# Which engine waits for the last store: SyncE or GpSimd

## Chip, cores, metric

One core of a Trainium2 chip. The metric is the device time of one execution in microseconds, the median of several runs. It is longer than the span that the profile shows (first to last instruction of the program): in this kernel by about 1.34 us.

## The reference

```python
def setup_inputs():
    batch, dim = 1024, 4096
    return {"x": randn(batch, dim) as float32, "y": randn(batch, dim) as float32}

def reference(x, y):
    z = x * y
    return (0.5 * z * (1 + np.tanh(np.sqrt(2 / np.pi) * (z + 0.044715 * z ** 3)))).astype(np.float32)
```

(Shortened.) Two arrays of 16.8 MB are read, multiplied, put through GELU, and one array of 16.8 MB is written.

## The kernel before

The data is cut into three pieces. SyncE issues every transfer; VectorE multiplies in place, ScalarE applies GELU in place; each transfer has a semaphore of its own. GpSimd has no part in it. What matters is the end:

```python
    # ... loads, multiplications and activations cut ...
    for i, (a, b) in enumerate(STORES):
        if i == 0:
            nc.sync.wait_ge(sem_y[-2], 16)
        nc.sync.wait_ge(sem_act, done[b])
        nc.sync.dma_start(out=columns(out, a, b), in_=xs[:, a:b]).then_inc(sem_o[i], 16)   # L113
    for i in range(len(STORES) - 1):
        nc.sync.wait_ge(sem_o[i], 16)                                                      # L115
    nums = sorted(s.num for s in [*sem_x, *sem_y, *sem_o[:-1], sem_mul, sem_act])
    assert nums == list(range(nums[0], nums[-1] + 1))
    nc.sync.sem_clear(range(nums[0], nums[-1] + 1))                                        # L118
    nc.sync.wait_ge(sem_o[-1], 16).then_inc(sem_o[-1], -16)                                # L119
```

While the last store is in flight SyncE already clears all the other semaphores; then it waits for the last store and takes its 16 off again. In the trace `sem_o[-1]` is semaphore 109.

## Time and profile before

| | |
|---|---|
| device time, median of 3 runs | 119.75 us (119.73 to 119.86) |
| device time and span of the profiled run | 119.64 and 118.3 us |
| landings of the two large stores | 98.970 and 116.763 us |
| last store: issue / landing | 97.487 / 118.270 us |
| last instruction of the program (SyncE, L119) ends | 118.304 us |
| last update of semaphore 2 | 119.757 us |

The prediction below shows the page's lines and reads them. By "landing" is meant the last of the sixteen increments that the trace has for each of the nine transfers. Two kinds of record matter. The views of instructions show the program's own instructions; the last wait appears there as 17 ns at 118.3 us, when it is over, although SyncE had waited 1.4 us. The semaphore records give number and time of the updates of semaphores, and they go on after the program's last instruction: five more steps of semaphore 2 (118.447 to 118.612 us), writes to nearly all other semaphores (118.572 to 119.177, 0.61 us), nine steps of semaphore 2 (119.401 to 119.757). These stand in the trace and not on the page. The records name no engine and no purpose.

A pass means here nine steps of semaphore 2, as from 119.401 to 119.757 us. The first pass at the end has its first four steps before the landing (2.147 to 97.658 us) and the five at 118.447 to 118.612 after it. The recorded texts call a pass "barrier", the order of its steps "serpentine", the time from one step to the next "hop" and the five blocks of writes "reset". Which engine makes which step, and that each writes a block, is the reading of the times.

### The profile page before, as it was taken

How to read it: one execution, taken by the hardware profiler on the slowest of the kernel's cores; microseconds unless marked ns; L12 is line 12 of the kernel's file. 1: busy time of each engine (PE TensorE's matmuls, PEld its weight loads, DVE VectorE, ACT ScalarE, POOL GpSimd, SP SyncE). 2: the span in 40 equal slices, each digit the busy share in tenths (PEclk: the TensorE clock that was granted, in tenths of full speed). 3: DMA queues.
4: the chain of work that ended last, by engine and by line, in shares of the span. 5: the costliest groups of instructions: out<-in, count | busy, mean ns of one | idle time of the engine just before them, and what ended most of it. 6: DMA issues, size and time to landing. Idle time of an engine off the chain costs nothing.

```text
span 118.3 us, 82 instructions
## 1 busy us (share of the span) xinstructions
DVE 35.2 (30%) x13; ACT 31.0 (26%) x14; POOL 0.2 (0%) x4
## 2 busy tenths in 40 slices
DVE  0000000000000069999920000059999940000000
ACT  3000000000000001977974000007998990000000
POOL 0000000000000000000000000000000000000000
DMA  9988899889988897797797797798899888977975
GB/s 375 556 355 355 355 643 421 355 355 421 643 355 355 355 654 327 327 654 327 327 654 327 327 654 327 327 576 355 355 576 487 355 355 368 613 327 327 654 327 222
DMA packets 1296, 50.33 MB, mean 425 GB/s; under 512 B 144, under 2 KB 144, under 8 KB 528
## 3 DMA queue, kind: packets, MB, share of 16 engines
q1 hardware_dynamic: 1296, 50.33, 98.8%
HBM read 33.55 MB, written 16.78 MB: 425 GB/s over the span
## 4 chain that ended last, share of the span: by engine, by line
DMA 53%; DVE 24%; ACT 3%; issue 1%; DVEq 0%
DMA ys<-in_y_dram 53%; DVE xs L96 24%; ACT xs L104 3%; DVEq L93 0%
## 5 line engine op out<-in xcount | busy, mean ns | idle before, releaser
L96 DVE TENSOR_TENSOR xs<-xs,ys 128x2048 f32<-128x2048 f32 (+3 forms) x13 | 35.2, 2778 | 60.7 <-DMA ys<-in_y_dram 60.7
L104 ACT ACTIVATE xs<-xs 128x2048 f32<-128x2048 f32 (+3 forms) x13 | 29.7, 2301 | 64.5 <-DVE xs L96 64.5
L104 ACT ACT_TABLE_LOAD x1 | 1.3, 1283 | 1.9 <-PEq L59 1.9
L134 POOL MEMSET const-bfloat16-1.0<- 128x1 bf16 x1 | 0.1, 102 | 0.0
L134 POOL MEMSET const-uint8-127<- 128x1 uint8 x1 | 0.1, 102 | 0.0
L134 POOL MEMSET const-float32-0.0<- 128x1 f32 x1 | 0.1, 99 | 0.2 <-issue 0.2
L134 POOL MEMSET const-float32-1.0<- 128x1 f32 x1 | 0.1, 99 | 0.0
## 6 DMA issues: line engine op xcount, KB each, us to landing
xs<-in_x_dram SPq DMA_DIRECT2D x1, 7552.0 KB, 57.9
ys<-in_y_dram SPq DMA_DIRECT2D x1, 7552.0 KB, 22.5
out_dram<-xs SPq DMA_DIRECT2D x1, 7552.0 KB, 20.4
xs<-in_x_dram SPq DMA_DIRECT2D x1, 640.0 KB, 3.6
ys<-in_y_dram SPq DMA_DIRECT2D x1, 640.0 KB, 19.7
out_dram<-xs SPq DMA_DIRECT2D x1, 640.0 KB, 20.8
xs<-in_x_dram SPq DMA_DIRECT2D x1, 22.6
ys<-in_y_dram SPq DMA_DIRECT2D x1, 40.4
```

Of the source, the lines that this page charges most:

```text
L96: nc.vector.tensor_mul(out=xs[:, c : c + w], in0=xs[:, c : c + w], in1=ys[:, r + c - a : r + c - a + w],).then_inc(sem_mul, 1)
L104: nc.scalar.activation(out=xs[:, c : c + w], in_=xs[:, c : c + w], func=GELU).then_inc(sem_act, 1)
L134: nc = _bacc.Bacc("TRN2", target_bir_lowering=False, num_devices=1)
```

## The change

The last wait goes from SyncE to GpSimd, which has been idle since the start (0.2 us of work there). The idea is that SyncE's program ends with the clear, and an engine with nothing else to do stands guard.

```diff
     nc.sync.sem_clear(range(nums[0], nums[-1] + 1))
-    nc.sync.wait_ge(sem_o[-1], 16).then_inc(sem_o[-1], -16)
+    nc.gpsimd.wait_ge(sem_o[-1], 16).then_inc(sem_o[-1], -16)
```

## The prediction

> **What bounds the kernel now.** I read the page first: span, busy shares, DMA queue and the DMA issues.
>
> ```profile
> span 118.3 us, 82 instructions
> DVE 35.2 (30%) x13; ACT 31.0 (26%) x14; POOL 0.2 (0%) x4
> ...
> q1 hardware_dynamic: 1296, 50.33, 98.8%
> HBM read 33.55 MB, written 16.78 MB: 425 GB/s over the span
> ...
> out_dram<-xs SPq DMA_DIRECT2D x1, 640.0 KB, 20.8
> ```
>
> The one DMA queue is busy for 98.8% of 16 engines' span. VectorE and ScalarE work for under a third of it, GpSimd for 0.2 us at the start. So the kernel is 50.33 MB through the DMA engines. The last store takes 20.8 us from issue to landing although it has only 640 KB, because it stands behind the two large stores.
>
> Next, the order of time at the end (start, duration, engine), then the waits of SyncE's sequencer (total, times, longest).
>
> ```profile
> 93.66 3.80 ACT L104 ACTIVATE xs<-xs 128x2048 f32<-128x2048 f32 x3 [0.29 <-DVE xs L96]
> 94.41 1.49 DVE L96 TENSOR_TENSOR xs<-xs,ys 128x1280 f32<-128x1280 f32 x1
> 96.33 1.49 SPq L113 DMA_DIRECT2D out_dram<-xs  x2
> ```
>
> ```profile
> SPq L115 <- DMA out_dram<-xs: 18.9, 1, 18.9
> ...
> SPq L119 <- SPq L119: 1.4, 1, 1.4
> ```
>
> All computing and issuing is over by 97.82 us (96.33 + 1.49). For the remaining 20.5 us SyncE only waits: 18.9 us for the large stores, then 1.4 us at line 119, the wait that the change moves. The view names SyncE itself as the releaser of that last wait, but the releaser must be the landing of the last store: the trace's semaphore records have its sixteenth increment at 118.270 us. The two lines in question, by source line (duration in ns min/median/max, first and last start):
>
> ```profile
> L118 SPq EVENT_SEMAPHORE_RANGE_CLEAR  x1: 44/44/44, 116.8 to 116.8; - x1
> ```
>
> ```profile
> L119 SPq EVENT_SEMAPHORE  x1: 17/17/17, 118.3 to 118.3; - x1
> ```
>
> The clear is already done 1.4 us before the last wait ends. Nothing the program does on SyncE follows the wait, so there is nothing to take off SyncE's path.
>
> The device time is longer than the span: the profiled execution took 119.64 us against 118.3, so about 1.34 us outside the program's own instructions belongs to the time. The views say nothing of it, but the trace keeps semaphore updates until 119.757 us. After the last instruction I see in them: semaphore 2 stepping five times (118.447, 118.492, 118.530, 118.564, 118.612); nearly all other semaphores written once each, in five blocks of about 50 that overlap, the first from 118.572 and the last until 119.177; then semaphore 2 stepping nine times (119.401 to 119.757). This is where the change can act.
>
> [...] the undisturbed last pass takes 119.757 − 119.401 = 0.356 us in nine steps. [...] Here the last increment is at 118.270 and the waiting instruction starts at 118.287, 17 ns later[...].
>
> **The change, part by part.**
> Removed from SyncE: one 17 ns instruction after a wait. Added to GpSimd: the same instruction; GpSimd has been idle since the start. Moved: nothing else. No transfer is issued at another time, no buffer comes free earlier, and the DMA stream that fixes 118.270 us is untouched. So the span should stay at 118.3, and only the way from 118.270 to the end can change.
>
> First, the order of the serpentine. Semaphore 2 steps at 2.147, at 97.576, 97.614, 97.658, and then not until 118.447. One engine arrives at 2.147, when only TensorE and GpSimd have finished. The second waits for ScalarE, whose last update is at 97.471. VectorE had finished earlier (last update 95.908) and did not step before ScalarE did, so it stands behind it. SyncE is fifth: its step follows the end of line 119. I read it as TensorE, ScalarE, GpSimd, VectorE, SyncE, and back: VectorE, GpSimd, ScalarE, TensorE. The hops of one engine repeat up and down: ScalarE 34, GpSimd 39 and 38, VectorE 44. That TensorE is the end post and GpSimd in the middle is a choice: the last hop is the slowest (47 ns), and TensorE's semaphore instructions are the slow ones, 51 ns against 17, in these lines:
>
> ```profile
> L59 POOLq EVENT_SEMAPHORE  x4: 17/17/17, 1.4 to 1.8; - x4
> ...
> L59 PEldq EVENT_SEMAPHORE  x2: 51/51/51, 1.5 to 1.9; - x2
> ```
>
> Before: SyncE is the turning point. The four ahead of it have stepped by 97.658, and only the way back remains: 118.612 − 118.447 = 0.165 us.
>
> After: GpSimd is the late one. TensorE and ScalarE have stepped; SyncE and VectorE have finished but may not step before GpSimd. So from GpSimd's step there is VectorE up, SyncE, VectorE down, GpSimd, ScalarE, TensorE. The undisturbed passes show that stretch: 119.757 − 119.473 = 0.284 us in the last one, and −0.302 to −0.003, so 0.299, in the one just before the program. Difference: 0.119 to 0.134 us later.
>
> Second, the way from landing to the late engine's step. SyncE: 17 ns to notice, 17 to the update at 118.304, 143 to its step at 118.447; in all 177. GpSimd, from its three waits at the start: 24 ns to notice (1.050 to 1.074, 1.378 to 1.402, 1.705 to 1.729) and 25 to the update (1.074 to 1.099 and so on). Then the step to the barrier: from a barrier step to the first semaphore write of its own block SyncE takes 118.572 − 118.447 = 125 ns and GpSimd, by the order above, 118.670 − 118.530 = 140. I estimate 143 × 140/125 = 160, and 140 as the low end. In all 189 to 209, so 12 to 32 ns more than SyncE.
>
> The sum is 0.131 to 0.166 us; I take 0.15. It goes to the end in full[...]. 119.75 + 0.15 = 119.90 us, 0.13% more.
>
> **The rivals.**
> A. SyncE, relieved of the wait, comes to the end early, and the closing work overlaps with the last store. For it: SyncE's own 143 ns from its last instruction to the barrier would be hidden. Against it: GpSimd has to pay the same step instead[...]. If GpSimd's step were free it would be about −0.143 + 0.12, nearly nothing; 119.6 at the very best, should GpSimd not stand in the way of the barrier.
> B. I have TensorE and GpSimd the wrong way round, and GpSimd opens and closes the serpentine. Then all nine steps come after the landing: 0.356 in place of 0.165, so +0.19 and the entry on top, about 119.96.
> C. Only the end of the program's own instructions counts, or noise covers it: 119.75 to 119.78. The 1.34 us between time and span speaks against the first; the spread of the three runs, 0.13 us, is as large as the effect, so the second can't be excluded in one comparison.
> D. A long wait of 116 us on GpSimd wakes slower than the short ones seen at its start. Nothing in the trace shows one; 0.1 us more would make 120.0.
>
> **Range and chances.** The centre is 119.90. Below it lie A, C and a draw at the low end of the spread; above it B, D and a draw at the high end. I give 119.74 to 120.06. Two per cent is 2.4 us, some sixteen times the effect and more than everything after the landing (1.49 us), so within 2% is all but sure: 0.98, with 0.01 on each side for something unseen in the DMA stream.
>
> **What would show it.** In the changed profile the last instruction should be GpSimd's semaphore instruction at 118.3 us, about 24 ns after the landing, with the span unchanged to within run-to-run scatter, and SyncE's last one the clear near 116.8. Semaphore 2 should step twice by 97.62 (TensorE, ScalarE) and seven times after the landing, where before it stepped four and five times; the first of the seven 0.19 to 0.21 us after the landing, and from there 0.284 to 0.299 to the last. One early step and eight late ones, or none and nine, would mean that I have the order wrong. If the landing itself moves by more than 0.1 us, the difference in time is the DMA's and not the wait's. A time below 119.7 would sink the argument.

The sum came to 0.131 to 0.166 us, of which 0.119 to 0.134 for the steps that remain and 0.012 to 0.032 for the way to the step; taken was 0.15. The 160 ns for GpSimd's step in it are an estimate. That the difference reaches the end in full was an assumption before the result.

## The result, and the profile after

The changed kernel takes 120.37 us (median of 6 runs, 120.25 to 120.46); the kernel before 119.78 us (6 runs, 119.73 to 120.46, of which five lie below 119.87). Ratios here are the mean time of one kernel's fast runs over that of the other's in the same rounds, so not quite the ratio of those medians: 1.0039, 95% interval 1.0017 to 1.0061. It is slower, by well under the 2% that would count, but four times as much as predicted and outside the predicted range.

The page of the changed kernel looks the same:

```profile
span 118.5 us, 82 instructions
DVE 35.2 (30%) x13; ACT 31.0 (26%) x14; POOL 0.2 (0%) x4
...
q1 hardware_dynamic: 1296, 50.33, 98.8%
HBM read 33.55 MB, written 16.78 MB: 425 GB/s over the span
...
out_dram<-xs SPq DMA_DIRECT2D x1, 640.0 KB, 20.8
```

The order of time at its end, then SyncE's waits (the line for 119 is gone), then lines 118 and 119:

```profile
93.86 3.80 ACT L104 ACTIVATE xs<-xs 128x2048 f32<-128x2048 f32 x3 [0.29 <-DVE xs L96]
94.61 1.49 DVE L96 TENSOR_TENSOR xs<-xs,ys 128x1280 f32<-128x1280 f32 x1
96.53 1.49 SPq L113 DMA_DIRECT2D out_dram<-xs  x2
```

```profile
SPq L115 <- DMA out_dram<-xs: 18.9, 1, 18.9
```

```profile
L118 SPq EVENT_SEMAPHORE_RANGE_CLEAR  x1: 44/44/44, 117.0 to 117.0; - x1
```

```profile
L119 POOLq EVENT_SEMAPHORE  x1: 17/17/17, 118.5 to 118.5; - x1
```

Every duration is that of before. All is shifted by about 0.2 us, and most of this offset is there long before the change acts: the first large load of x landed at 22.992 us before and 23.144 after. That is scatter of the transfers, as a repeat shows below.

The difference is in the semaphore records after the last landing. In each pass semaphore 2 makes nine steps, which the prediction reads as up through the engines and back down. These are the times in us of the steps of the first pass, with the last landing and the last update of semaphore 109; the bar separates the steps before the landing from those after it:

```
          landing  update   | steps of semaphore 2
before    118.270  118.304  | 2.147 97.576 97.614 97.658 | 118.447 118.492 118.530 118.564 118.612
after     118.452  118.502  | 2.147 97.772 | 119.055 119.098 119.122 119.218 119.258 119.292 119.339
```

From the landing to the end of the pass (called the tail below): 118.612 − 118.270 = 0.342 us before, 119.339 − 118.452 = 0.887 us after, so 0.545 more. What follows, the writes and the second pass, is unchanged: 119.757 − 118.612 = 1.145 and 120.487 − 119.339 = 1.148 us. Two steps come early and seven late, as predicted, and those seven take 0.284 us, as predicted. But the first of the seven comes 0.553 us after GpSimd's update; SyncE's came 0.143 us after its own.

### The profile page after: what moved, and what is told of

The parts are those of the page before. It is cut to its first block, busy times and chain, and to the rows that moved or that the text cites. A ratio compares the mean times of both kernels' runs of the same rounds, so it can differ in the third digit from the quotient of the medians.

```text
span 118.5 us, 82 instructions
## 1 busy us (share of the span) xinstructions
DVE 35.2 (30%) x13; ACT 31.0 (26%) x14; POOL 0.2 (0%) x4
## 4 chain that ended last, share of the span: by engine, by line
DMA 53%; DVE 24%; ACT 3%; issue 1%; DVEq 0%
DMA ys<-in_y_dram 53%; DVE xs L96 24%; ACT xs L104 3%; DVEq L93 0%
## 5 line engine op out<-in xcount | busy, mean ns | idle before, releaser
L96 DVE TENSOR_TENSOR xs<-xs,ys 128x2048 f32<-128x2048 f32 (+3 forms) x13 | 35.2, 2779 | 60.9 <-DMA ys<-in_y_dram 60.9
```

Source lines behind the costliest of these rows:

```text
L96: nc.vector.tensor_mul(out=xs[:, c : c + w], in0=xs[:, c : c + w], in1=ys[:, r + c - a : r + c - a + w],).then_inc(sem_mul, 1)
```

## The experiments

Theory T1: on its way from its program's last instruction to its step of semaphore 2 GpSimd has some 0.4 us of its own that SyncE has not, whatever it waited for. Rivals: the moved clear or wait costs in itself (T2), the half microsecond belongs to the pass itself, when the others have arrived (T3), GpSimd wakes slowly after 116 us of idleness (T4), every engine but SyncE pays it (T5), an instruction has to be fetched at the end of the program, and the cost depends on where that lies (T6). All runs gave correct results.

### GpSimd waits, but for an earlier store

```diff
-    for i in range(len(STORES) - 1):
-        nc.sync.wait_ge(sem_o[i], 16)
-    nums = sorted(s.num for s in [*sem_x, *sem_y, *sem_o[:-1], sem_mul, sem_act])
+    nc.sync.wait_ge(sem_o[0], 16)
+    nums = sorted(s.num for s in [*sem_x, *sem_y, sem_o[0], sem_mul, sem_act])
 ...
     nc.sync.sem_clear(range(nums[0], nums[-1] + 1))
+    nc.gpsimd.wait_ge(sem_o[1], 16).then_inc(sem_o[1], -16)
     nc.sync.wait_ge(sem_o[-1], 16).then_inc(sem_o[-1], -16)
```

> SyncE keeps the wait for the last store; GpSimd waits only for the second store (lands near 116.8 us) and SyncE clears before that. Theory T1 (GpSimd's own way from its last instruction to the barrier takes about 0.55 us, whatever it waited for): GpSimd's step of semaphore 2 comes 0.55 us after its update, near 117.4, hidden behind the last store; from the last landing to the end of the first barrier pass 0.34 us as before, device time that of before (119.8 us, ratio 1.000). Theory T2 (moving the clear or any wait off SyncE costs in itself): time near 120.3. Theory T3 (the 0.55 us belongs to the pass of the barrier, when GpSimd holds the others up after they arrived): GpSimd's step follows its update within 0.16 us, near 117.0.

Measured: 119.79 us against 119.76 before, ratio 0.9998 (0.9983 to 1.0013). Line 118 of this run's kernel, by source line:

```profile
L118 POOLq EVENT_SEMAPHORE  x1: 17/17/17, 116.9 to 116.9; - x1
```

GpSimd's update is at 116.912 us and its step of semaphore 2 at 117.465: 0.553 us again, with nobody to wait for and nobody behind it in a hurry. The last store lands at 118.377, so the step is long over; from landing to the end of the pass it takes 0.339 us. T2 and T3 fall. The half microsecond is GpSimd's own and costs nothing as long as GpSimd is not the last.

### Two waits in a row on GpSimd

```diff
-    nc.sync.wait_ge(sem_o[-1], 16).then_inc(sem_o[-1], -16)
+    nc.gpsimd.wait_ge(sem_o[-1], 16)
+    nc.gpsimd.wait_ge(sem_o[-1], 16).then_inc(sem_o[-1], -16)
```

> As the changed kernel, but GpSimd waits for the last store twice in a row, and only the second wait takes the 16 off. T1 (own way to the barrier after the program's last instruction): the second wait starts about 0.08 us after the first, and the step of semaphore 2 still comes 0.55 us after its update; time 0.08 us above the changed kernel. T4 (slow waking of the sequencer after a wait of 116 us): the second wait starts 0.4 us or more after the first, and the step then follows within 0.16 us; time as the changed kernel.

The profile still has 82 instructions: the two waits had been merged into one with two conditions (43 ns in place of 17), so the spacing of the two was not to be seen. It took 120.41 us, the step came 0.553 us after the update once more. For T4 this run decides nothing.

### GpSimd at work shortly before the end

GpSimd waits for the second store, zeroes a few elements of the spent y buffer, then waits for the last store.

```diff
     nc.sync.sem_clear(range(nums[0], nums[-1] + 1))     # without sem_o[1], as in the first experiment
-    nc.sync.wait_ge(sem_o[-1], 16).then_inc(sem_o[-1], -16)
+    nc.gpsimd.wait_ge(sem_o[1], 16).then_inc(sem_o[1], -16)
+    nc.gpsimd.memset(ys[:, 0:8], 0.0)
+    nc.gpsimd.wait_ge(sem_o[-1], 16).then_inc(sem_o[-1], -16)
```

> GpSimd waits for the second store, sets 8 elements a partition of the spent y buffer to zero, then waits for the last store[...]. T1: the step still comes 0.55 us after the update, device time 120.3 to 120.4 us as the changed kernel. T4[...]: the step follows within 0.16 to 0.3 us, time 119.9 to 120.1 us.

In order of time, just before the end:

```profile
117.00 0.10 POOL L119 MEMSET ys<- 128x8 f32 x1 [116.57 <-POOLq L118]
```

After 116.57 us without work the first wait's update is at 116.903 us and the memset starts at 116.997, 94 ns later: no slow waking. And although GpSimd's memset ended only 1.3 us before the landing, its step comes at 118.983, 0.553 us after its last update at 118.430. T4 falls (the run with drains behind the wait, below, leaves no idle time at all and has a long step too, 524 ns). The time was 120.56 us (120.31 to 120.59, ratio 1.0059), above the changed kernel's; three of its four runs have spans of 118.6 to 118.7, so that excess lies inside the span. The tail is 0.888 us.

### The last wait on ScalarE, VectorE, TensorE

One word differs each time: `nc.scalar`, `nc.vector` or `nc.tensor` in the place of `nc.sync` in the last line.

> The last wait on ScalarE. T1 (the long step is GpSimd's own, the rest is the place in the serpentine): step about 0.105 to 0.14 us after the update, then 0.322 us to the end of the pass (119.757-119.435 of the last pass of before); from landing to the end of the pass 0.46 to 0.50 us, 0.12 to 0.16 us over before: device time 119.9 to 119.95. Theory T5 (any engine other than SyncE pays the half microsecond): landing to end of pass 0.9 us, time 120.35.

> The last wait on VectorE. Law so far (time from landing to the end of the first barrier pass = notice + update + the engine's own step to the barrier + the hops that remain from its place): notice and update about 45 to 50 ns, own step 0.165 to 0.175 us (its way from barrier to reset in the run of before was 144 ns where ScalarE's was 120, and ScalarE's measured step was 145), hops from VectorE's step on 0.24 us (119.757-119.517 in before's last pass). Landing to end of pass 0.45 to 0.47 us against 0.342 before: device time 119.87 to 119.90. The rival, that GpSimd alone is slow for its place and VectorE, its neighbour, pays nothing at all, would give 0.34 us and 119.77.

> The last wait on TensorE, the end post of the serpentine: all nine steps come after the landing. Notice and update 0.07 to 0.1 us, own step 0.22 to 0.27 us (TensorE's other ways of this kind were 0.218 to 0.224), then the whole pass, 0.356 us: landing to end of pass 0.65 to 0.72 us, device time 120.1 to 120.15. If TensorE's own step is as long as GpSimd's (0.55), 1.0 us and 120.4.

The last one, by source line:

```profile
L119 PEldq EVENT_SEMAPHORE  x1: 51/51/51, 118.6 to 118.6; - x1
```

From the semaphore records, in ns, with the first two rows from the kernels before and after:

| last wait on | landing to update | update to own step | own step to end of pass | sum | time minus span, mean (us) | median time (us), ratio |
|---|---|---|---|---|---|---|
| SyncE | 34 | 143 | 165 | 342 | 1.34 | 119.76 and 119.83 in the two rounds |
| GpSimd | 50 | 553 | 284 | 887 | 1.87 | 120.37, 1.0039 |
| VectorE | 58 | 172 | 241 | 471 | 1.46 | 119.92, 1.0008 |
| ScalarE | 45 | 145 | 325 | 515 | 1.52 | 120.01, 1.0016 |
| TensorE | 92 | 266 | 358 | 716 | 1.68 | 120.19, 1.0035 |

The third column of numbers depends on the place in the pass, and the steps counted give the order that the prediction had inferred: with the wait on ScalarE one step is early and eight are late, with VectorE three and six, with TensorE none and nine. Of the first column, 17 ns (SyncE) to 28 ns (VectorE, TensorE) pass before the waiting instruction starts. The second column, the engine's way to its own step, is 143 to 266 ns for four engines and 553 for GpSimd alone: T5 falls. ScalarE came out 0.015 us above the expected tail (0.515 against 0.46 to 0.50) and TensorE at its upper end; the three times lay 0.02 to 0.06 us above the expected ones. The intervals of the ratios for VectorE (0.9995 to 1.0022) and ScalarE (1.0001 to 1.0031) reach down to no difference or nearly so; their order is read from the records, not from the times.

### Empty instructions that never reached the chip

Three runs put empty instructions (`nop`) around the wait: 300 before it on GpSimd, 8 after it on GpSimd, 8 after it on SyncE as control.

```diff
+    for _ in range(300):
+        nc.gpsimd.nop()
     nc.gpsimd.wait_ge(sem_o[-1], 16).then_inc(sem_o[-1], -16)
```

```diff
     nc.gpsimd.wait_ge(sem_o[-1], 16).then_inc(sem_o[-1], -16)     # and the same with nc.sync
+    for _ in range(8):
+        nc.gpsimd.nop()
```

> The changed kernel with 300 empty instructions on GpSimd before its wait[...]. T6 (GpSimd's 0.55 us are an instruction fetch at the end of the program, so they depend on where that lies): the step after the update differs clearly from 0.553 us (0.15 us, or 1 us and more). T1 as a fixed part of GpSimd's closing sequence: 0.553 us again to within 0.02, device time 120.35 to 120.4 as the changed kernel.

> The changed kernel with 8 empty instructions on GpSimd after its wait. If GpSimd's long step is serial work of its closing sequence, it starts after the last of them: from the end of the last empty instruction to the step of semaphore 2 again about 0.5 us, and landing to the end of the pass longer than 0.887 us by the time of the eight (some 0.1 to 0.6 us). If the step is a wait for something that runs beside[...], the eight hide in it and 0.887 us stays.

> The kernel before with the same 8 empty instructions on SyncE after its wait, as the control: from the last of them to SyncE's step 0.12 to 0.15 us as before; landing to the end of the pass 0.342 us plus the eight.

The first line of the first one's page:

```profile
span 118.5 us, 82 instructions
```

82 instructions, as in the kernels without them, and none with their line in the trace: the empty instructions had been dropped on the way. The three are repeats of the kernels that they start from (tails 0.887, 0.887 and 0.340 us; medians 120.47, 120.34, 119.82) and say nothing of T6. Had I looked only at the step (0.553 us, as T1 expected), the first would have passed as a confirmation.

### The changed kernel once more

> The changed kernel again, to separate landing from tail: time minus span 1.85 us against 1.34 for before in every run, so 0.51 us, and spans that overlap with before's to within 0.1 us. If the wait on GpSimd also slows the transfers, the spans stay above before's by 0.15 us or more in the mean.

120.28 us in the median of 5 runs against 119.83 before (9 runs), ratio 1.0040 (1.0027 to 1.0054). The mean span is 118.44 us against 118.48 before; time minus span 1.88 against 1.34. So no slowing of the transfers is seen, and the 0.2 us between the first two profiles was scatter: the profile of the kernel before was an early one, 118.3 us against the mean of 118.48. The whole effect lies after the program: 0.54 us, the 0.545 of the records.

### Without the subtraction after the wait

```diff
-    nc.sync.wait_ge(sem_o[-1], 16).then_inc(sem_o[-1], -16)
+    nc.gpsimd.wait_ge(sem_o[-1], 16)
```

> The changed kernel without the subtraction of 16 after the wait[...]. If the subtraction on GpSimd is what is slow, landing to the end of the pass falls from 0.887 to 0.5 us or less; if the closing sequence is, it stays at 0.86 to 0.89 us.

The tail is 0.856 us, 31 ns less than 0.887. Two runs gave 120.31 and 120.71 us, the latter with a span of 118.9. The subtraction is not what is slow.

### Real instructions before and after the wait

Drains do nothing for the result either, but they reach the chip: the profile lists each one, 34 ns long on GpSimd and 7 on SyncE. The next three runs are the intended ones.

```diff
+    for _ in range(300):
+        nc.gpsimd.drain()
     nc.gpsimd.wait_ge(sem_o[-1], 16).then_inc(sem_o[-1], -16)
```

```diff
     nc.gpsimd.wait_ge(sem_o[-1], 16).then_inc(sem_o[-1], -16)     # and the same with nc.sync
+    for _ in range(8):
+        nc.gpsimd.drain()
```

> The changed kernel with 300 drains on GpSimd before its wait, over long before the end. They must show in the profile: 382 instructions in place of 82. Fetch at the end of the program: the step after GpSimd's update differs clearly from 0.553 us. Fixed closing work: 0.553 us within 0.02, landing to end of pass 0.887 us, time 120.3 to 120.5.

> The changed kernel with 8 drains on GpSimd after its wait (90 instructions). Serial closing work: from the last drain to the step about 0.5 us or more, and landing to end of pass 0.887 us plus the eight, some 0.3 to 0.6 us more. Something that runs beside from the wait on: the eight hide, 0.887 us stays. Slow waking after the wait: the first drain starts 0.4 us or more after the wait.

> Control: the kernel before with 8 drains on SyncE after its wait. From the last drain to SyncE's step 0.12 to 0.16 us; landing to end of pass 0.342 us plus the eight.

The first line of the page and the drains of each (300 before the wait on GpSimd; 8 after it on GpSimd; 8 after it on SyncE):

```profile
span 119.2 us, 382 instructions
```

```profile
L120 POOLq DRAIN  x300: 34/34/184, 1.9 to 21.0; - x150
```

```profile
L121 POOLq DRAIN  x8: 34/34/34, 118.4 to 118.9; - x8
```

```profile
L121 SPq DRAIN  x8: 7/7/7, 118.6 to 119.0; - x8
```

With 300 instructions more in GpSimd's program the step comes 119.814 − 119.256 = 0.558 us after the update: it does not depend on where the program ends, so T6 falls in the form above. What the 0.55 us are it does not show, but its trace has stops of a similar length. The drains start 61 ns apart, but twice, 128 drains apart, GpSimd is held up: the drain at 5.520 us starts 407 ns after the one before it and takes 172 ns, the one at 13.733 us 350 and 184 ns. That is 0.48 and 0.44 us lost, close to the 0.41 us by which GpSimd's step is longer than SyncE's. The records of instruction fetches come only 4.2 to 4.7 us after these hold-ups. So it settles nothing that the trace of the changed kernel has no such record after the program. No run puts a hold-up like these at the end.

With 8 drains behind the wait on GpSimd, the first drain starts 56 ns after the update (118.378 to 118.434), the last ends at 118.894, and the step comes at 119.418: 524 ns later. The tail is 1.374 us, 0.487 more than 0.887, and eight drains at the measured distance of 60.9 ns are 0.487. Nothing of them is hidden. On SyncE the last drain ends at 119.031 and the step comes at 119.152, 121 ns later; the tail is 0.766 us. So the long step is serial time after whatever GpSimd's program does last, and in the same test it is 0.40 us longer than SyncE's. The times follow: 120.83 us with the drains on GpSimd, 120.25 on SyncE (two runs each), both 0.46 us above the kernels without them (120.37 and 119.79).

The 300 drains also cost something not asked for: 121.33 us, with spans of 119.2 and 119.3. The first large load of x already landed at 23.887 us, 0.74 us later than in the changed kernel, and two more fetches of 8192 bytes of instructions, 309 ns each, stand in the trace at 10.2 and 17.9 us. Of the sixteen increments of that landing fifteen are in by 23.075 us and the last comes at 23.887; in the changed kernel all sixteen come between 22.675 and 23.144. So one of the sixteen increments is late and not all of them. Whether it has to do with the fetches is not shown: the records name no DMA engine, and no run separates the fetches from the drains.

## Why the prediction was wrong

**Right:** the transfers and the span, which stay (118.44 against 118.48 us in the repeat). **Right:** the order of the steps up to the late engine. Rival B would have put one step early or none; the runs on the five engines have four (SyncE), three (VectorE), two (GpSimd), one (ScalarE) and no step (TensorE) early. **Right:** the hops, 0.284 us measured against 0.284 to 0.299. **Right:** notice and update on GpSimd, 25 + 25 ns against 24 + 25. **Right:** that the whole tail goes to the end in full (from the end of the pass to the last record 1.145 us before, 1.148 after).

**Wrong:** the step that the prediction put as "I estimate 143 × 140/125 = 160". It measured 553 ns. The scaling used the 140 ns from a step to a block of writes, both GpSimd's by the reading, as a stand-in for the way from its program's end to its step, because the latter could not be seen before: GpSimd's step hid behind ScalarE's at 97.576 us. With 553 in place of 160 the prediction's own sum becomes 50 + 553 + 284 − 342 = 545 ns, and the records show 545. With 119.75 that makes 120.30; measured 120.37 and 120.28.

That only the time after the landing changes, and the sign, were right, and one term was mis-sized by 0.39 us. The range was too narrow because it treated a term without any observation as one known to 20 ns; rival D had allowed 0.1 us for it, and for another reason. Waking is not it: the runs with an early wait, with a memset and with drains show that (0.553, 0.553 and 0.524 us). A hint stood in the trace before: in a pass before the program, too, the step that the rest of the pass waits for is the third, GpSimd's by this order, 0.82 us after the second (0.55 to 1.45 us in the sixteen traces). Whether it is the same cost no run shows.

Two smaller points of the prediction do not hold. VectorE's two hops in the undisturbed last pass are 44 and 97 ns by the order read, not equal, so the last hop, 47 ns, is not the slowest of that pass either; the sum is untouched, because its 0.284 us was read from that whole pass. And the sign that a landing moved by more than 0.1 us makes the difference the DMA's was too strict: it moved by 0.18 us between the two profiles, while spans of the unchanged kernel alone went from 118.3 to 118.6.

What stays open is what GpSimd does in those 0.4 us. No instruction is on record after the program's last, no semaphore is updated in that time, and no transfer is on record. Whether it is the same thing that held up the train of 300 drains twice (0.48 and 0.44 us) was not tested. Shown is only that the time is serial, is GpSimd's alone, has a fixed length (0.553 to 0.558 us in eight runs with the update as the last instruction) and depends neither on idleness, nor on the subtraction, nor on the length of the program.

No run beats the kernel before beyond its scatter. The table says why: SyncE's way to its step is short (143 ns; ScalarE's is 145), and with SyncE last four of the nine steps are already made and the other five take 165 ns, the least of the five engines.

## What to carry to other kernels

The program's last instruction is not the end of the measured time: which engine finishes last decides how long it takes from the last landing to the end of the pass, here 0.34 us for SyncE and 0.89 for GpSimd. On this evidence, from one kernel and worth 0.5 us, SyncE should wait for the last transfer and the others finish early, where their own way to their step is hidden (GpSimd's 0.553 us in the first experiment: 119.79 against 119.76 us). And where a term of an estimate was hidden behind something in the profile, give it a range of its own instead of borrowing a number from a neighbouring operation; and check in the profile that an instruction put in for an experiment is really there.
